# Writing the relative-bias rows from 96 partitions, and loading the compressed keys' bias from a table in steps of 16

## The chip, the core and the metric

One core of a Trainium2 chip runs the whole kernel. The metric is the device time of one execution in microseconds; lower is better. The core has TensorE (PE in the profile; PEld is its weight load), VectorE (DVE), ScalarE (ACT), GpSimd (POOL) and SyncE (SP), which here only issues DMAs: every DMA of this kernel stands in SP's one queue, in program order, and the transfers run on 16 DMA engines.

## The reference

Two decoder layers over 512 tokens of width 1024, batch 1, float32. Layer 0 is native sparse attention with 12 heads (compressed blocks, selected blocks, sliding window, gated and added) beside a 4-head cross-attention into `mem` (256 tokens); layer 1 is block-sparse attention with the same 12 heads beside the same kind of cross-attention. After each comes a gated convolutional FFN (width 2816). All softmax logits of the 12 heads get a bias that depends on the distance between query and key alone:

```python
def rel_bucket(dist):                  # 32 buckets over the distance
    ...
lg = einsum('bqgjd,bngd->bqgjn', qc, k_cmp) * scale + head_bias(rel_bucket(dist_c))   # 31 compressed keys
p_c = masked_softmax(lg, (dist_c >= 0)...)      # dist_c = t - (16 n + 31)
lg = einsum('bqgjd,bgqkd->bqgjk', qc, ks) * scale + bias_s                             # 512 keys
...
x = layer_norm(ALPHA * x + mix, ...)
```

The bias table `rel_bias` is 32 buckets x 12 heads. A compressed key n ends at position 16 n + 31, and there are 31 of them.

## The kernel before

It is written in a tile framework whose scheduler sets the order of the instructions on each engine from its own estimate of their times; priorities and buffers decide, not the order of the code alone. Every float32 product is made of three matmuls on values split in a high and a low part (`mm3`): ACT makes the high part (`hi`, line 231), DVE or POOL the low part (`lo`, lines 234 and 262). Weights come in units of 128 x 512 float32 (256 KB) into the tile `raw`, of which there are 5 (`unit`, lines 257 and 259), and are split from there.

How the bias gets to the logits: `tables` multiplies a one-hot matrix (33 x 640; row 32 stands for keys in the future) with `rel_bias`, once for the 12 heads, which gives one row of 640 values for each head, and ACT copies it to the tile `rt` (12 partitions, in a `kj` buffer). `bias_out` writes each row 32 times to `bias_rows` in DRAM (12 x 32 x 640 float32, 983 KB), by one DMA that reads each of the 12 partitions 32 times. `bias_tile` then loads, for a head, a tile `T` of 128 x 512 in which each partition's row is shifted by one: four DMAs of 32 partitions, 64 KB each (line 357). In layer 0, `cmp_bias` loads such a tile for each of the 12 heads as well, only to copy every 16th column of it (31 columns) on POOL into the table `C`, which `compressed_group` adds to the logits of the compressed keys (line 350).

The start of the program, in which all of this lies: x is transposed (`nat`, line 245), the K and V inputs of the compression are projected (`psS<-xh`), `stacked` copies them to two `p` tiles, the weights of V and of the gates (164 columns, tiles `p`, `v`, `pc`) are split, K is projected (`psmm<-xh`, 128 x 512) and then V and the gates in four blocks of tokens (`psmm<-p,xh`, later `psS<-p,xh`, 24 matmuls each). `mem_kv` transposes `mem` in two halves (`kj<-in_mem_dram`, two loads of 512 KB; high and low part in the tile `o`) and makes K and V of the cross-attention (`psS<-o,hi` and `psS<-hi,o`) from 8 weight units. `compress` runs twice over 8 units each (`in_a_cmp_w_k_dram`, `in_a_cmp_w_v_dram`; `psPT<-hi,p`). Then come the two cross-attention pairs (`psS<-xh,hi`, 24 matmuls of 512 columns) and the 12 heads of layer 0. The call order in `layer0` is: `compress` for K, gates, `compress` for V, `bias_out`, `cmp_bias` for 12 heads, `mem_pair`.

Of the kernel before, what the change touches and what calls it, by code (L numbers as in the profile page):

```python
# [10 lines left out]
F = mybir.dt.float32  # L11
R = mybir.dt.float32r
I32 = mybir.dt.int32
AF = mybir.ActivationFunctionType
# [7 lines left out]
NH = 12  # L22
# [11 lines left out]
GC = math.sqrt(2.0 / math.pi)  # L34
NREV = 640
REP = 32
OFF = (0, 128, 384, 768)


def _bucket(n):  # L40
    n = np.maximum(n, 0)
    nf = np.maximum(n, 1).astype(np.float32)
    large = 16 + (np.log(nf / np.float32(16)) / np.float32(math.log(128 / 16))
                  * np.float32(16)).astype(np.int32)
    return np.where(n < 16, n, np.minimum(large, 31))


def _onehot():
    dist = 511 - np.arange(NREV)
    oh = np.zeros((33, NREV), np.float32)  # L50
    oh[np.where(dist >= 0, _bucket(dist), 32), np.arange(NREV)] = 1.0
    return oh


SBUF = dict(raw=(5, 512), hi=(4, 1024), lo=(4, 1024), nat=(4, 1024), xh=(1, 4096), xl=(1, 4096),
# [127 lines left out]
class Trunk:  # L183
# [118 lines left out]

    def setup(self):
        nc, a = self.nc, self.a
        self.oh = self.al("kj")
        self.rb = self.one.tile([33, NH], F, name="rb")
        nc.vector.memset(self.rb[32:33, :], -BIG)
        self.nat = [self.al("nat") for _ in range(NT)]
        x = lambda tb, c0, c1: nc.sync.dma_start(self.nat[tb][:, c0:c1], a["x"][0, tb * 128:tb * 128 + 128, c0:c1])
        x(0, 0, 512)  # L310
        x(0, 512, D)
        nc.sync.dma_start(self.rb[0:32, :], a["rel_bias"])
        nc.sync.dma_start(self.oh[0:33, 0:NREV], a["onehot"])
        self.wkv = self.al("kj")
        nc.sync.dma_start(self.wkv.rearrange("p (k m) -> p k m", k=KC),
                          a["a_w_in"][0][:, 768:896].rearrange("(k p) m -> p k m", p=128))
        for tb in range(1, NT):
            x(tb, 0, D)
        self.ident = self.one.tile([128, 128], F, name="ident")
        make_identity(nc, self.ident)  # L320
        self.i2 = self.one.tile([64, 32], F, name="i2")
        nc.vector.tensor_add(self.i2, self.ident[0:64, 0:32], self.ident[0:64, 32:64])
        self.cw = self.one.tile([128, 2, NF * 3], F, name="cw")
        self.cb = self.one.tile([128, 2, NF], F, name="cb")
        self.new_xT()
        for tb in range(NT):
            self.to_xT(tb)

    def tables(self):
        nc, oh, rb = self.nc, self.oh, self.rb  # L330
        rt = self.al("kj")[0:NH, 0:NREV]
        for c0, c1 in ((0, 512), (512, NREV)):
            ps = self.pj()
            self.mm(ps[0:NH, 0:c1 - c0], rb, oh[0:33, c0:c1], True, True)
            nc.scalar.activation(rt[0:NH, c0:c1], ps[0:NH, 0:c1 - c0], AF.Copy, scale=-1.0)
        self.B = self.dr.tile([NH, REP, NREV], F, name="bias_rows")
        self.rt = rt
        self.aux = self.al("v")
        self.C = self.aux[:, 0:NH * 56].rearrange("p (h j) -> p h j", h=NH)
        nc.gpsimd.memset(self.C[:, :, 31:56], BIG)  # L340

    def bias_out(self):
        nc, a = self.nc, self.a
        nc.sync.dma_start(self.B, self.rt.unsqueeze(1).to_broadcast([NH, REP, NREV]))
        nc.sync.dma_start(self.cw, a["conv_w"])
        nc.sync.dma_start(self.cb, a["conv_b"])

    def cmp_bias(self, h):
        t = self.bias_tile(h)
        self.nc.gpsimd.tensor_copy(self.C[:, h, 0:31], t[:, 16:512].rearrange("p (j s) -> p j s", s=16)[:, :, 15])  # L350

    def bias_tile(self, h, c0=0):
        t = self.al("T")
        for p in range(0, 128, REP):
            src = bass.AP(tensor=self.B.tensor, offset=self.B.offset + h * REP * NREV + 127 - p + c0,
                          ap=[[NREV - 1, REP], [1, 512 - c0]])
            self.nc.sync.dma_start(t[p:p + REP, c0:512], src)
        return t
# [40 lines left out]
    def causal(self, q2, k2, T, gate, v, O, start, stop, qs=range(NT)):  # L399
# [5 lines left out]
        P = self.al("p")  # L405
        L = {i: P[:, OFF[i]:OFF[i] + 128 * (i + 1)] for i in qs}
        nm, sm = self.small(4), self.small(4)
# [413 lines left out]
    def layer0(self):  # L821
        nc, a = self.nc, self.a
        w = a["a_w_in"][0]
# [19 lines left out]
        ps = self.projT2(self.pj(), (v3(sh, 128), v3(sl, 128)))  # L843
# [5 lines left out]
        for j in range(2):  # L849
            d = (slice(None), slice(None), slice(64 * j, 64 * j + 64))  # L850
            src = v3(raw[j], 128)[:, :, 0:64]
# [9 lines left out]
        ps = self.projT(self.pj(), (v3(kh, 128), v3(kl, 128)))  # L861
# [17 lines left out]
        for tb in range(NT):  # L879
            ps = self.pj()  # L880
            t = slice(128 * tb, 128 * tb + 128)
# [9 lines left out]
        nc.vector.memset(self.G[0:31, 0, :, 0], 0.0)  # L891
        self.compress(t2v, pev, a["a_cmp_w1_v"][0], w2v, False)
        self.bias_out()
        for h in range(NH):
            self.cmp_bias(h)
        self.mem_pair(K2m, V2m, wq0, 0)
        self.mem_pair(K2m, V2m, self.cols(w, 1316), 1)

        q = {}
# [157 lines left out]
```

## Time and profile before

| | |
|---|---|
| median of 3 runs | 1258.29 us (1257.38 to 1259.96) |
| the profiled execution's own time | 1259.36 us |
| its span (first to last instruction) | 1257.4 us |
| mean granted TensorE clock | 0.985 of full speed |
| PE / PEld / DVE / ACT / POOL busy | 96% / 82% / 67% / 50% / 19% of the span |
| moved by DMA | 142.73 MB, 114 GB/s over the span |

The span is what the trace covers; the device time holds 2.0 us more around it. PE's matmuls are pipelined and their ends are modelled, so that a busy PE may still run at half its clock or wait for little things; the trace's stretches show where.

### The profile page before, as it was taken

The page shows a single profiled execution, that of the slowest core. Times are in us where ns is not written, and L with a number is a line of the kernel's source. Part 1 is how long each engine was busy: PE and PEld are TensorE (multiplying, and loading weights), DVE is VectorE, ACT ScalarE, POOL GpSimd, SP SyncE. Part 2 cuts the span into 40 slices and gives each one's busy share as a digit, 9 for nine tenths or more (in the row PEclk, how much of TensorE's full clock was granted, in tenths as well). Part 3 has the DMA queues.
Part 4 walks back from the last instruction along what each step waited for, and adds up shares of the span by engine and source line. Part 5 has one row for each costly group of instructions (what it writes and reads, how often), then busy time and mean ns, then how long its engine had stood idle before and what let it go on. Part 6 is the DMA issues. An engine that isn't in the chain of part 4 may idle for free.

```text
span 1257.4 us, 18606 instructions
## 1 busy us (share of the span) xinstructions
PE 1210.6 (96%) x6304; PEld 1032.2 (82%) x6304; DVE 847.6 (67%) x1861; ACT 628.4 (50%) x1347; POOL 237.8 (19%) x332
## 2 busy tenths in 40 slices
PE   7789999999999999999999999998899999999996
PEld 6778788888888888888879888887888888888875
DVE  6446897998755566468695665548875556646967
ACT  6458776672533334336543876456253433433652
POOL 0245553552000000000002445334200000000004
PEclk9899999999999999999999999999899999999998
DMA  9782110321534544336513223234154344433531
GB/s 234 209 202 80 46 43 24 79 84 35 168 118 121 148 124 128 101 118 209 176 59 102 75 77 90 79 93 118 34 160 125 118 140 129 127 107 117 170 108 67
DMA packets 173944, 142.73 MB, mean 114 GB/s; under 512 B 11768, under 2 KB 142200, under 8 KB 173849
## 3 DMA queue, kind: packets, MB, share of 16 engines
q1 hardware_dynamic: 173848, 141.55, 38.6%
q8 instruction: 50, 0.82, 0.3%
q14 instruction: 46, 0.37, 0.1%
HBM read 138.42 MB, written 3.08 MB: 113 GB/s over the span
## 4 chain that ended last, share of the span: by engine, by line
PE 84%; DVE 7%; DMA 3%; ACT 3%; issue 1%; SPq 1%; POOL 0%; DVEq 0%; POOLq 0%; ACTq 0%
PE psmm L237 41%; PE psS L237 28%; PE psPT L237 6%; PE psO L237 4%; PE psPT L245 4%; DVE pt L234 1%; DMA kj<-in_mem_dram 1%; DVE p L412 1%; DMA raw<-in_ffn_w_out_dram 1%; DVE nat L672 1%; ACT p L417 1%; ACT kj L231 1%; DVE nat L679 1%; ACT pt L231 1%; DVE nat L622 1%
## 5 line engine op out<-in xcount | busy, mean ns | idle before, releaser
L231 ACT ACTIVATE hi<-raw 128x512 fp32r<-128x512 f32 x370 | 216.4, 624 | 286.9 <-PE psS L237 158.0
L262 DVE TENSOR_TENSOR lo<-raw,hi 128x512 fp32r<-128x512 f32 x270 | 178.8, 693 | 108.1 <-ACT hi L231 106.4
L237 PE MATMUL psmm<-xh,lo 128*128 128x512 f32 (+1 forms) x560 | 212.0, 379 | 0.0
L237 PE MATMUL psmm<-xh,hi 128*128 128x512 f32 (+1 forms) x560 | 211.8, 379 | 0.0
L237 PE MATMUL psmm<-xl,hi 128*128 128x512 f32 (+1 forms) x560 | 211.7, 378 | 0.0
L262 POOL TENSOR_TENSOR lo<-raw,hi 128x512 fp32r<-128x512 f32 x68 | 88.8, 1328 | 438.9 <-DVE st L638 357.2
L237 PE MATMUL psS<-xh,hi 128*128 128x512 f32 (+1 forms) x408 | 151.9, 373 | 2.6 <-ACT G L888 2.6
L237 PE MATMUL psS<-xl,hi 128*128 128x512 f32 (+1 forms) x408 | 151.3, 372 | 0.1
L237 PE MATMUL psS<-xh,lo 128*128 128x512 f32 (+1 forms) x408 | 151.1, 370 | 0.0
L237 PEld LDWEIGHTS psmm<-xh,lo 128*128 128x128 f32 x560 | 105.4, 188 | 18.9
L237 PEld LDWEIGHTS psmm<-xl,hi 128*128 128x128 f32 x560 | 105.4, 188 | 18.7
L237 PEld LDWEIGHTS psmm<-xh,hi 128*128 128x128 f32 x560 | 105.4, 188 | 18.7 <-DVE qq L365 0.2
L237 PE MATMUL psmm<-hi,kj 128*128 128x512 f32 x328 | 114.3, 401 | 3.2 <-ACT kj L231 2.2
L417 ACT ACTIVATE p<-p,s 128x128 f32<-128x128 f32 (+3 forms) x144 | 79.9, 556 | 33.4 <-DVE s L412 32.6
L421 POOL TENSOR_SCALAR p<-p,s 128x128 f32<-128x128 f32 (+3 forms) x144 | 74.2, 532 | 99.7 <-DVE s L388 49.7
L237 PEld LDWEIGHTS psS<-xh,hi 128*128 128x128 f32 x408 | 77.8, 191 | 15.6 <-ACT G L888 2.8
L237 PEld LDWEIGHTS psS<-xl,hi 128*128 128x128 f32 x408 | 77.7, 191 | 13.4 <-DVE xl L234 0.5
L237 PEld LDWEIGHTS psS<-xh,lo 128*128 128x128 f32 x408 | 77.7, 190 | 13.0
L412 DVE CUSTOM_DVE_ANT_0 p<-psS,T 128x128 f32<-128x128 f32 (+3 forms) x144 | 66.1, 484 | 24.0 <-PE psS L237 20.5
L234 DVE TENSOR_TENSOR pt<-psPT,pt 128x512 fp32r<-128x512 f32 (+2 forms) x124 | 73.5, 606 | 8.4 <-ACT pt L231 7.6
L231 ACT ACTIVATE pt<-psPT 128x512 fp32r<-128x512 f32 (+2 forms) x124 | 64.1, 530 | 27.1 <-PE psPT L245 15.2
L237 PEld LDWEIGHTS psmm<-hi,kj 128*128 128x128 f32 x328 | 61.5, 189 | 16.1 <-ACT kj L231 2.6
(331 smaller groups left out, 2334.4 us busy)
## 6 DMA issues: line engine op xcount, KB each, us to landing
raw<-in_ffn_w_in_dram SPq DMA_DIRECT2D x176, 256.0 KB, 3.2
raw<-in_ffn_w_out_dram SPq DMA_DIRECT2D x152, 256.0 KB, 3.0
T<-bias_rows SPq DMA_DIRECT2D x144, 64.0 KB, 2.0
raw<-in_shared_w_kv_dram SPq DMA_DIRECT2D x24, 256.0 KB, 3.2
raw<-in_a_w_out_dram SPq DMA_DIRECT2D x16, 256.0 KB, 3.0
raw<-in_b_w_in_dram SPq DMA_DIRECT2D x16, 256.0 KB, 3.2
raw<-in_b_w_out_dram SPq DMA_DIRECT2D x16, 256.0 KB, 3.1
raw<-in_a_w_in_dram SPq DMA_DIRECT2D x14, 256.0 KB, 3.8
```

The source lines that it names most:

```text
L231: self.nc.scalar.activation(dst, src, AF.Copy)
L234: self.nc.vector.tensor_sub(dst, src, hi.bitcast(F))
L237: self.nc.tensor.matmul(o, l, r, start=start, stop=stop, skip_group_check=more)
L245: self.nc.tensor.transpose(o, i, self.ident)
L262: eng.tensor_sub(l[:, c], raw, h[:, c].bitcast(F))
L412: nc.vector.tensor_tensor_reduce(L[i], dst[i], T[:, 384 - 128 * i:512], op0=ALU.add, op1=ALU.min, scale=1.0, scalar=BIG, accum_out=nm[:, i ...
L417: nc.scalar.activation(L[i], L[i], AF.Exp, bias=nm[:, i:i + 1], scale=-1.0, accum_out=sm[:, i:i + 1])
L421: nc.gpsimd.tensor_scalar(L[i], L[i], r[:, i - qs[0]:i - qs[0] + 1], 1.0, op0=ALU.mult, op1=ALU.mult)
L622: nc.vector.scalar_tensor_tensor(self.nat[tb][:, sl], self.nat[tb][:, sl], ALPHA if first else 1.0, ps, op0=ALU.mult, op1=ALU.add)
L672: nc.vector.scalar_tensor_tensor(x[:, c], x[:, c], mu, gt[:, c], op0=ALU.subtract, op1=ALU.mult)
L679: eng.scalar_tensor_tensor(x[:, c], x[:, c], y, bt[:, c], op0=ALU.mult, op1=ALU.add)
```

## The change

The one-hot table gets 608 more columns: 16 groups of 38, in which column n of group m stands for the distance 511 - (46 - m + 16 n), so that a row of it is the bias in steps of 16. `tables` now makes two things: the rows as before, but for 96 columns of weights (each head 8 times, `rbs`, copied by DVE), so that they lie on 96 partitions; and for the 12 heads the 608 values in steps of 16, in two `pt` buffers. `bias_out` writes the latter to DRAM (`bias_16`, two DMAs from 12 partitions, 29 KB), writes `bias_rows` from 96 partitions with 4 copies of each, and loads the table `C` by 8 DMAs (16 partitions each, 12 heads x 31 values, runs of 124 bytes). `cmp_bias` is gone, with its 48 loads of `T` and 12 copies on POOL. The one-hot matrix moves from a `kj` to a `p` buffer.

```diff
--- before.py
+++ after.py
@@ -34,6 +34,8 @@
 GC = math.sqrt(2.0 / math.pi)
 NREV = 640
 REP = 32
+COPIES = 8
+NCMP = 38
 OFF = (0, 128, 384, 768)
 
 
@@ -49,7 +51,8 @@
     dist = 511 - np.arange(NREV)
     oh = np.zeros((33, NREV), np.float32)
     oh[np.where(dist >= 0, _bucket(dist), 32), np.arange(NREV)] = 1.0
-    return oh
+    by_16 = 46 - np.arange(16)[:, None] + 16 * np.arange(NCMP)
+    return np.concatenate([oh, oh[:, by_16.reshape(-1)]], 1)
 
 
 SBUF = dict(raw=(5, 512), hi=(4, 1024), lo=(4, 1024), nat=(4, 1024), xh=(1, 4096), xl=(1, 4096),
@@ -302,7 +305,7 @@
 
     def setup(self):
         nc, a = self.nc, self.a
-        self.oh = self.al("kj")
+        self.oh = self.al("p")
         self.rb = self.one.tile([33, NH], F, name="rb")
         nc.vector.memset(self.rb[32:33, :], -BIG)
         self.nat = [self.al("nat") for _ in range(NT)]
@@ -310,7 +313,7 @@
         x(0, 0, 512)
         x(0, 512, D)
         nc.sync.dma_start(self.rb[0:32, :], a["rel_bias"])
-        nc.sync.dma_start(self.oh[0:33, 0:NREV], a["onehot"])
+        nc.sync.dma_start(self.oh[0:33, 0:NREV + 16 * NCMP], a["onehot"])
         self.wkv = self.al("kj")
         nc.sync.dma_start(self.wkv.rearrange("p (k m) -> p k m", k=KC),
                           a["a_w_in"][0][:, 768:896].rearrange("(k p) m -> p k m", p=128))
@@ -328,26 +331,37 @@
 
     def tables(self):
         nc, oh, rb = self.nc, self.oh, self.rb
-        rt = self.al("kj")[0:NH, 0:NREV]
-        for c0, c1 in ((0, 512), (512, NREV)):
-            ps = self.pj()
-            self.mm(ps[0:NH, 0:c1 - c0], rb, oh[0:33, c0:c1], True, True)
-            nc.scalar.activation(rt[0:NH, c0:c1], ps[0:NH, 0:c1 - c0], AF.Copy, scale=-1.0)
+        n, m = NH * COPIES, 16 * NCMP
+        rbs = self.one.tile([33, NH, COPIES], F, name="rbs")
+        nc.vector.tensor_copy(rbs, rb.unsqueeze(2).to_broadcast([33, NH, COPIES]))
+        self.rt = self.al("kj")[0:n, 0:NREV]
+        self.ru = self.al("pt")[0:NH], self.al("pt")[0:NH, 0:m - 512]
+        for dst, w, c in ((self.rt[:, 0:512], rbs, 0), (self.rt[:, 512:NREV], rbs, 512),
+                          (self.ru[0], rb, NREV), (self.ru[1], rb, NREV + 512)):
+            if w is rbs:
+                w = rbs.rearrange("p h r -> p (h r)")
+            ps = self.pj()[0:dst.shape[0], 0:dst.shape[1]]
+            self.mm(ps, w, oh[0:33, c:c + dst.shape[1]], True, True)
+            nc.scalar.activation(dst, ps, AF.Copy, scale=-1.0)
         self.B = self.dr.tile([NH, REP, NREV], F, name="bias_rows")
-        self.rt = rt
+        self.B16 = self.dr.tile([NH, m], F, name="bias_16")
         self.aux = self.al("v")
         self.C = self.aux[:, 0:NH * 56].rearrange("p (h j) -> p h j", h=NH)
         nc.gpsimd.memset(self.C[:, :, 31:56], BIG)
 
     def bias_out(self):
         nc, a = self.nc, self.a
-        nc.sync.dma_start(self.B, self.rt.unsqueeze(1).to_broadcast([NH, REP, NREV]))
+        n = REP // COPIES
+        nc.sync.dma_start(self.B16[:, 0:512], self.ru[0])
+        nc.sync.dma_start(self.B16[:, 512:16 * NCMP], self.ru[1])
+        nc.sync.dma_start(self.B.rearrange("h (r n) c -> (h r) n c", n=n),
+                          self.rt.unsqueeze(1).to_broadcast([NH * COPIES, n, NREV]))
+        for q in range(8):
+            src = bass.AP(tensor=self.B16.tensor, offset=self.B16.offset + 7 - q,
+                          ap=[[NCMP, 16], [16 * NCMP, NH], [1, 31]])
+            nc.sync.dma_start(self.C[16 * q:16 * q + 16, :, 0:31], src)
         nc.sync.dma_start(self.cw, a["conv_w"])
         nc.sync.dma_start(self.cb, a["conv_b"])
-
-    def cmp_bias(self, h):
-        t = self.bias_tile(h)
-        self.nc.gpsimd.tensor_copy(self.C[:, h, 0:31], t[:, 16:512].rearrange("p (j s) -> p j s", s=16)[:, :, 15])
 
     def bias_tile(self, h, c0=0):
         t = self.al("T")
@@ -891,8 +905,6 @@
         nc.vector.memset(self.G[0:31, 0, :, 0], 0.0)
         self.compress(t2v, pev, a["a_cmp_w1_v"][0], w2v, False)
         self.bias_out()
-        for h in range(NH):
-            self.cmp_bias(h)
         self.mem_pair(K2m, V2m, wq0, 0)
         self.mem_pair(K2m, V2m, self.cols(w, 1316), 1)
```

The scheduler gives the start of the program another order. SP's queue before, from the write of the bias rows on (`kj_364` is the second half of `mem`, `T_857` the first head's tile for `cmp_bias`):

```order
L344 DMA bias_rows<-kj_209 384x1x640
L345 DMA cw<-in_conv_w_dram 128x132
L346 DMA cb<-in_conv_b_dram 128x44
L448 DMA kj_364<-in_mem_dram 128x1024
L257 DMA raw_475<-in_a_w_mem_kv_dram 128x2x256
L357 DMA T_857<-bias_rows 32x512 x2
L257 DMA raw_481<-in_a_w_mem_kv_dram 128x2x256
L357 DMA T_857<-bias_rows 32x512
L257 DMA raw_485<-in_a_w_mem_kv_dram 128x2x256
```

SP's queue now, from the first of the three bias writes on (`bias_227` is `bias_16`, `kj_375` the second half of `mem`, `v_228` holds the table `C`, `T_1259` and `T_1482` are the tiles of the first two attention heads):

```order
L355 DMA bias_227<-pt_212 12x512
L356 DMA bias_227<-pt_213 12x96
L357 DMA bias_rows<-kj_211 384x1x640
L363 DMA cw<-in_conv_w_dram 128x132
L364 DMA cb<-in_conv_b_dram 128x44
L462 DMA kj_375<-in_mem_dram 128x1024
L260 DMA raw_486<-in_a_w_mem_kv_dram 128x2x256
L362 DMA v_228<-bias_227 16x12x31
L260 DMA raw_492<-in_a_w_mem_kv_dram 128x2x256
L260 DMA raw_496<-in_a_w_mem_kv_dram 128x2x256
L362 DMA v_228<-bias_227 16x12x31 x7
L371 DMA T_1259<-bias_rows 32x512
```

The loads of `T` between the weight units are gone but for those of heads 0 and 1; two small writes stand ahead of the large one, and eight loads of `C` stand ahead of the units of the compression.

ACT before, from the split of the weights of V and the gates back to the copies of `stacked` (`p_279`, `p_282`; `p_287` is the split weight, `o_347` the transposed `mem`, `raw_382` and on the units of `mem_kv`):

```order
L231 ACTIVATE p_279<-psS_230 64x512
L231 ACTIVATE p_279<-psS_230 64x511
L231 ACTIVATE p_282<-psS_230 64x512
L231 ACTIVATE p_282<-psS_230 64x511
L231 ACTIVATE p_287<-kj_225 128x8x64
L231 ACTIVATE p_287<-kj_226 128x8x64
L231 ACTIVATE p_287<-v_217 128x8x36
L231 ACTIVATE o_347<-psPT_350 128x4x128
L231 ACTIVATE hi_380<-raw_382 128x512
L231 ACTIVATE o_347<-psPT_357 128x4x128
L231 ACTIVATE hi_380<-raw_386 128x512
```

ACT now, at the same place (`p_290`, `p_293` and `p_298` are the same three tiles, `o_358` the transposed `mem`, `raw_393` and on the same units):

```order
L234 ACTIVATE hi_391<-raw_393 128x512
L234 ACTIVATE o_358<-psPT_361 128x4x128
L234 ACTIVATE o_358<-psPT_368 128x4x128
L234 ACTIVATE hi_391<-raw_397 128x512
L234 ACTIVATE hi_435<-raw_437 128x512
L234 ACTIVATE p_290<-psS_241 64x512
L234 ACTIVATE p_290<-psS_241 64x511
L234 ACTIVATE p_293<-psS_241 64x512
L234 ACTIVATE p_293<-psS_241 64x511
L234 ACTIVATE p_298<-kj_236 128x8x64
L234 ACTIVATE p_298<-kj_237 128x8x64
L234 ACTIVATE p_298<-v_228 128x8x36
```

Five instructions that stood behind the split weight (two halves of the transposed `mem`, three weight units) stand ahead of the copies of `stacked` now; DVE's order is changed in the same way.

## Rows read from the trace of the kernel before

**Rows 1.** The page's first line and its chain of work that ended last, as shares of the span by engine.

```profile
span 1257.4 us, 18606 instructions
...
PE 84%; DVE 7%; DMA 3%; ACT 3%; issue 1%; SPq 1%; POOL 0%; DVEq 0%; POOLq 0%; ACTq 0%
```

**Rows 2.** The same chain in order of time, at the start of the program: start, duration (both us), what.

```profile
25.11 12.14 DMA kj<-in_mem_dram
...
60.76 6.03 DMA raw<-in_a_cmp_w_v_dram
...
68.97 7.29 PE psS L237 x24
```

**Rows 3.** Waits of PE between 18 and 100 us: engine, line, what it waited for, us in total, times, longest.

```profile
PE psPT L245 <- DMA kj<-in_mem_dram: 8.5, 1, 8.5
PE psS L237 <- ACT G L888: 2.6, 1, 2.6
PE psPT L237 <- ACT p L547: 0.8, 1, 0.8
PE psS L237 <- DVE kj L234: 0.5, 1, 0.5
```

**Rows 4.** Busy time in stretches of 2 us: stretch, its length, PE, PEld, DVE, ACT, POOL busy (x instructions), granted PE clock, DMA share of 16 engines, GB/s.

```profile
24.00:26.00 2.00, 2.00 (x10) 1.68 (x9) 2.00 (x7) 2.00 (x5) 0.00 (x0) 1.00 0.72 79
...
28.00:30.00 2.00, 0.85 (x8) 0.70 (x7) 2.00 (x5) 1.39 (x4) 0.00 (x0) 1.00 0.70 77
...
34.00:36.00 2.00, 0.00 (x0) 0.00 (x0) 0.00 (x0) 0.00 (x0) 0.00 (x0) 0.50 0.91 319
...
38.00:40.00 2.00, 2.00 (x10) 1.54 (x8) 0.86 (x2) 1.49 (x3) 0.00 (x0) 0.50 0.87 264
40.00:42.00 2.00, 2.00 (x11) 2.00 (x12) 1.66 (x3) 1.50 (x4) 0.23 (x1) 0.62 1.00 280
...
70.00:72.00 2.00, 2.00 (x6) 1.61 (x5) 0.76 (x6) 0.39 (x2) 0.23 (x1) 0.50 0.34 83
72.00:74.00 2.00, 2.00 (x9) 1.59 (x9) 0.00 (x0) 0.00 (x0) 0.23 (x1) 0.94 0.66 135
```

**Rows 5.** SP in order of time: start, duration, line, what it issued, how many.

```profile
15.05 4.19 SPq L257 DMA_DIRECT2D raw<-in_a_w_mem_kv_dram  x5
19.34 0.92 SPq L344 DMA_DIRECT2D bias_rows<-kj  x1
...
20.88 4.13 SPq L346 DMA_DIRECT2D cb<-in_conv_b_dram  x1
25.11 4.43 SPq L448 DMA_DIRECT2D kj<-in_mem_dram  x1
29.64 3.65 SPq L257 DMA_DIRECT2D raw<-in_a_w_mem_kv_dram  x1
34.56 0.80 SPq L357 DMA_DIRECT2D T<-bias_rows  x2
```

**Rows 6.** DMA issues between 34 and 76 us: what, how many, KB each, median us from issue to landing.

```profile
T<-bias_rows SPq DMA_DIRECT2D x48, 64.0 KB, 2.2
...
raw<-in_a_cmp_w_v_dram SPq DMA_DIRECT2D x8, 256.0 KB, 6.2
```

**Rows 7.** PE in order of time: start, duration of the row, what, [idle before]. The matmuls of the tables (x2: float32 goes through in two passes), the first transposes, the first block of V and the gates, the transposes of the second half of `mem`.

```profile
5.55 1.86 PE L237 MATMUL psS<-kj,rb 33*12 33x512 f32 x2
7.21 0.63 PE L237 MATMUL psmm<-kj,rb 33*12 33x128 f32 x2
8.69 2.82 PE L245 MATMUL psPT<-ident,nat 128*128 128x128 f32 x12 [0.84 <-DMA nat<-in_x_dram]
...
26.05 0.24 PE L237 MATMUL psmm<-p,xh 128*128 128x164 f32 x1
...
28.58 0.28 PE L237 MATMUL psmm<-p,xl 128*128 128x164 f32 x1
37.39 1.94 PE L245 MATMUL psPT<-ident,kj 128*128 128x128 f32 x8 [8.53 <-DMA kj<-in_mem_dram]
```

**Rows 8.** ACT in order of time, same columns: the copies of `stacked`, the split of the weights of V and the gates, weight units, K; and the last DVE instruction of that split.

```profile
19.89 2.42 ACT L231 ACTIVATE p<-psS 64x512 f32<-64x512 f32 x4 [1.01 <-PE psS L237]
22.34 1.16 ACT L231 ACTIVATE p<-kj 128x512 fp32r<-128x512 f32 x2
23.40 0.43 ACT L231 ACTIVATE p<-v 128x288 fp32r<-128x288 f32 x1
...
26.37 1.67 ACT L231 ACTIVATE hi<-raw 128x512 fp32r<-128x512 f32 x3
27.93 1.19 ACT L231 ACTIVATE kl<-psmm 64x512 fp32r<-64x512 f32 x2
...
24.96 0.28 DVE L234 TENSOR_TENSOR pc<-v,p 128x108 fp32r<-128x108 f32 x1
```

**Rows 9.** POOL's wait for the tiles of `cmp_bias`, between 28 and 80 us.

```profile
POOL v L350 <- DMA T<-bias_rows: 34.8, 12, 10.4
```

**Rows 10.** DMA issues from 15.9 to 16.4 us: what, how many, KB each, median us from issue to landing.

```profile
raw<-in_a_w_mem_kv_dram SPq DMA_DIRECT2D x2, 256.0 KB, 5.6
```

**Rows 11.** SP's issues of loads with short runs (L869: 256 bytes, L872: 64 bytes): start, duration, line, what, how many.

```profile
5.40 2.92 SPq L869 DMA_DIRECT2D v<-in_a_cmp_w_k_dram  x2
...
14.10 0.43 SPq L872 DMA_DIRECT2D v<-in_pe_v_dram  x1
```

## The prediction

> **What bounds the kernel now.** The chain of work that ended last is 84% PE [rows 1], so over the whole span the kernel is bound by matmuls, which this change does not touch but for the tables. What it can move is the start, where the same chain, read in order of time, leaves PE: 12.14 us on the load of the second half of `mem`, 6.03 us on weight units of the second compression [rows 2]. The waits of PE in that stretch say what this costs: 8.5 us for `mem`, then 0.8 and 2.6 us behind ACT, which stood in its own order behind weight units that had not landed, and 0.5 us behind DVE [rows 3].
>
> Why is `mem` late? SP issued the write of the bias rows at 19.34 us, and the first load that needs them starts at 34.56, when the write has landed: 15.2 us for 983 KB [rows 5]. While it alone is under way the DMA engines are busy 0.70 to 0.72, near 12 of 16, and move 77 to 79 GB/s; a stretch of loads right behind it has 319 GB/s [rows 4]. Behind the write, SP's next issues take 4.13, 4.43 and 3.65 us [rows 5], and the second half of `mem`, issued into this, takes the 12.14 us. After that come 48 loads of `T`, 3.1 MB, between the weight units [rows 6]; POOL waits 34.8 us for them [rows 9], which hurts nobody, but the units behind them are late, the ones of the second compression with 6.2 us to landing [rows 6].
>
> The waits also cost clock. PE is at half its clock (the granted clock is 0.50) when it comes back at 37.4, and the mean of 0.62 in 40 to 42 says that this lasts to about 41.5: 4.1 us of work at half speed, some 2.1 us lost. After the second wait the clock is 0.50 in 70 to 72 and 0.94 in 72 to 74, so from 68.97 to about 72.2: 1.6 us lost [rows 2, 4].
>
> **What the change removes.** The sum of the above, without the 0.5 us for DVE, which the change leaves: 8.5 (wait for `mem`) + 2.1 (clock) + 0.8 + 2.6 (waits behind ACT) + 1.6 (clock) = 15.6 us. Not all of the two waits behind ACT can go, since some latency of ACT and DVE stays once the units are there; I keep 0.7 of it. So 14.9 us are to be had if `mem` and the units come in time.
>
> Does `mem` come in time? The five units ahead of the write have landed by 17.9 + 5.6 = 23.5 us, with the last of them issued about 17.9 (1.35 us before SP's next row at 19.34) and the landing of their like [rows 5, 10]. How fast the write is from 96 partitions no row shows. Bounds: 983 KB at 319 GB/s, 3.1 us, and, if only the number of busy engines goes from 12 to 16, 78 x 16/12 = 104 GB/s, 9.5 us [rows 4]. Behind it 512 KB of `mem` need 1.6 us at 319 GB/s, so they land between 28 and 35 us. PE wants them behind the first block of V and the gates, which ends at 28.9 in the profile [rows 7] and, by what is added below, at about 31.5. I take the fast end, since the slow write's rate is far below anything that the engines do in the other stretches, and what is common to its packets is that 12 partitions are read 32 times each.
> [...]
>
> And the units? The 8 loads of `C` stand ahead of the compression's first unit, 190 KB in runs of 124 bytes. An issue of short runs took 0.43 us when the queue was free and 2.92 / 2 = 1.5 us when it was full [rows 11], so 3.4 to 12 us for all eight against 48 issues of `T` removed, at 0.80 / 2 = 0.4 us [rows 5] 19 us of SP and 3.1 MB / 319 GB/s = 9.9 us of transfer. SP comes to the compression's units at about 33 us then; ACT takes the first of them only behind K of the cross-attention, about 41. So the cover is some 5 us, and I put the loads of `C` at nothing.
>
> **What it adds and moves.** Two more matmul pairs for the table in steps of 16: by their likes 1.86 and, for 96 of 128 columns, 0.5 us; the 0.84 us that PE waits for x behind the tables take part of it [rows 7]. PE is then busy to 28.9 without a break, so 1.4 us later (bounds 1.2 and 2.4). ACT gets 0.7 us there, beside PE. The 80 KB more of one-hot table are 0.3 us of transfer, inside this.
>
> ACT and DVE are the price of the new order. Five ACT instructions now stand ahead of the copies of `stacked`, of which the last needs a unit that lands near 22.5; at 1.67 / 3 = 0.56 us each the copies start at about 23.4 instead of 19.89. The split weight is then ready on ACT at 27.3 instead of 23.83, and on DVE 1.4 us later, at 28.7 instead of 25.24 [rows 8]. PE comes to the first block that needs it at 26.05 + 1.4 = 27.5 [rows 7]: a new wait of 1.2 us (bounds 0.5 and 2.5). Behind it on ACT stand three units and one copy at 0.56 and K in two parts of 1.19 us, 4.6 us, before the transposed second half of `mem` [rows 8]: at 31.9 it begins, at 33 both halves are out, while PE is done with the transposes at 32.1. Another 1.0 us (bounds 0 and 2.5). Who waits behind: the cross-attention's K on PE, and all that follows.
>
> Sum: 14.9 - 1.4 - 1.2 - 1.0 = 11.3 us. Against the profiled execution's own 1259.4 us this is 1248.1; that run is 1.1 us over the median of the runs, from which it is 1247.0. I give 1247. From some 95 us on PE is full in both, and nothing there hangs on the bias but the tiles of the heads, of which each comes from DRAM as before; I take the gain to go through to the end.
>
> **The rivals.**
> - *The loads of `C` clog the queue* (the other side). If each issue is held as the ones behind the slow write were, about 4 us [rows 5], eight take 33 us instead of 3.4; SP comes to the compression's units at 62, PE waits for them from about 46 on, some 20 us against 11.3 gained: 1267. It turns at an issue of (11.3 + 5) / 8 + 0.4 = 2.5 us. Against it: 1.5 us is the dearest that a load of short runs took, in a full queue [rows 11]. [...]
> - *The write gets only 16/12 faster, or the new ACT and DVE order costs its upper bounds.* `mem` is 3 us later than PE wants it, and the clock may fall for another 1.5 us; or 2.5 + 2.5 us of new waits and the fallen clock. Gain 5 to 8: about 1251.
> - *The write is as slow as before* (the rows are read at the same rate, whatever the partitions): `mem` lands at 37 again, and what is left are the waits after it, 0.8 + 2.6 + 1.6 - 0.7 = 4.3, less 1.4 for the tables: 1255.4.
> - *All of it is won*: the tables hidden, no new wait on ACT: 14.9, 1243.4.
>
> **How the numbers follow.** My forecast (gain 9 to 14) 0.56; the second rival 0.22; the third 0.07; all won 0.06; the first, or another wait that eats the gain, 0.09. The range 1243 to 1254 leaves out the slow write, the clogged queue and the end of the best case, some 2 in 10. 0.2%, what a measurement of this kernel can tell, is 2.5 us. All cases but the last are faster by that, though the third barely: faster 0.89; same 0.04; slower 0.07.
>
> **What would show it.** Right: the write lands about 5 us after the units ahead of it, SP's issues behind it take under 1.5 us, PE's wait for `mem` is gone and the clock stays at 1.00 between 30 and 42; small new waits of PE behind DVE's `v` or ACT's `o` between 27 and 34; the first cross-attention pair (24 matmuls of 512) starts near 59 instead of 68.97 and takes 5.5 instead of 7.29 us. Wrong: a wait of PE for weight units of the compression, loads of `C` that take over 2 us to issue, a granted clock of 0.50 behind one of the new waits, or an early gain that is given back before 250 us.

## The result, and the profile after the change

| | before | after |
|---|---|---|
| device time, median | 1258.99 us (4 runs, 1257.38 to 1259.96) | 1247.49 us (4 runs, 1246.38 to 1248.12) |
| ratio | | 0.991, 95% interval 0.9894 to 0.9926 |
| profiled execution, own time | 1259.36 us | 1246.38 us |
| its span | 1257.4 us | 1244.6 us |

The change makes the kernel 11.5 us faster by the medians; 1247.0 was predicted. The two profiled executions lie 12.8 us apart in span, and all that follows on places is read from them.

The first lines of the page of the changed kernel, which answer to [rows 1]: span, and busy time, share of the span and instructions of PE.

```profile
span 1244.6 us, 18522 instructions
PE 1207.8 (97%) x6308; PEld 1029.9 (83%) x6308; DVE 847.2 (68%) x1862; ACT 629.2 (51%) x1349; POOL 235.0 (19%) x320
```

Waits of PE from 18 to 100 us, which answer to [rows 3]: engine, line, what it waited for, us in total, times, longest.

```profile
PE psS L240 <- DVE kj L237: 0.8, 1, 0.8
PE psS L240 <- ACT o L234: 0.8, 1, 0.8
PE psmm L240 <- DVE v L237: 0.6, 1, 0.6
```

The wait of 8.5 us for `mem` and the two behind ACT (2.6 and 0.8) are gone. Two of the three that are left are the new ones that the prediction named, behind the split weight `v` and behind the transposed `mem` in `o`; the third was there before with 0.5.

SP in order of time, as in [rows 5]: start, duration, line, what it issued, how many.

```profile
17.91 1.33 SPq L260 DMA_DIRECT2D raw<-in_a_w_mem_kv_dram  x1
...
20.18 0.68 SPq L357 DMA_DIRECT2D bias_rows<-kj  x1
...
21.57 1.81 SPq L364 DMA_DIRECT2D cb<-in_conv_b_dram  x1
23.47 1.38 SPq L462 DMA_DIRECT2D kj<-in_mem_dram  x1
24.95 0.38 SPq L260 DMA_DIRECT2D raw<-in_a_w_mem_kv_dram  x1
...
26.88 3.83 SPq L362 DMA_DIRECT2D v<-bias  x7
```

DMA issues between 18 and 34 us: what, how many, KB each, median us from issue to landing.

```profile
bias_rows<-kj SPq DMA_DIRECT2D x1, 960.0 KB, 6.5
...
cb<-in_conv_b_dram SPq DMA_DIRECT2D x1, 22.0 KB, 5.6
```

The write is issued at 20.18 and has landed at 26.7; it took 15.2 us before. The issues behind it, which took 4.13, 4.43 and 3.65 us, take 1.81, 1.38 and 0.38. The stretches of 2 us, with the columns of [rows 4], say the same from the side of the rate and of the clock:

```profile
24.00:26.00 2.00, 2.00 (x10) 1.69 (x9) 1.72 (x5) 1.94 (x5) 0.00 (x0) 1.00 1.06 293
26.00:28.00 2.00, 1.63 (x8) 1.13 (x6) 2.00 (x7) 2.00 (x6) 0.00 (x0) 1.00 0.82 298
...
32.00:34.00 2.00, 1.40 (x12) 1.40 (x13) 1.97 (x4) 1.21 (x3) 0.61 (x1) 1.00 0.63 160
...
40.00:42.00 2.00, 1.26 (x11) 1.10 (x10) 1.10 (x3) 1.48 (x5) 0.40 (x1) 1.00 0.48 145
...
sum 36.00, PE 33.84 PEld 32.23 DVE 24.41 ACT 23.91 POOL 4.15; mean PE 2.12 PEld 2.01 DVE 1.53 ACT 1.49 POOL 0.26
```

293 and 298 GB/s stand where 77 to 79 stood, and the granted clock, 0.50 from 32 to 40 before, is 1.00 throughout. The sum is over 24 to 60 us: PE is idle for 36.00 - 33.84 = 2.16 us there, the three waits above (0.83 + 0.77 + 0.56).

The chain that ended last, in order of time, as in [rows 2]:

```profile
42.09 5.98 PE psS L240 x48
...
57.77 5.67 PE psS L240 x24
```

The first cross-attention pair, at 68.97 with 7.29 us before, starts 11.2 us earlier and is 1.6 us shorter: 12.8 us are won by its end, and the span ends 12.8 us earlier. In between, the first FFN begins at 301.8 instead of 315.5 and the last output goes out at 1241.8 instead of 1254.6. So the gain is 13.7 us at the FFN, and 0.9 of it is lost again by the end: 0.3 by a longer wait of PE at the end of the second FFN (1.17 us for 0.84), the rest I did not trace.

### The profile page after: what moved, and what is told of

The parts are those of the page before. It is cut to its first block, busy times and chain, and to the rows that moved or that the text cites. A ratio compares the mean times of both kernels' runs of the same rounds, so it can differ in the third digit from the quotient of the medians.

```text
span 1244.6 us, 18522 instructions
## 1 busy us (share of the span) xinstructions
PE 1207.8 (97%) x6308; PEld 1029.9 (83%) x6308; DVE 847.2 (68%) x1862; ACT 629.2 (51%) x1349; POOL 235.0 (19%) x320
## 3 DMA queue, kind: packets, MB, share of 16 engines
q1 hardware_dynamic: 173260, 138.70, 37.4%
## 4 chain that ended last, share of the span: by engine, by line
PE 87%; DVE 7%; ACT 3%; DMA 1%; issue 1%; POOL 0%; SPq 0%; DVEq 0%; ACTq 0%; POOLq 0%
PE psmm L240 42%; PE psS L240 29%; PE psPT L240 7%; PE psO L240 5%; PE psPT L248 4%; DVE pt L237 1%; DMA raw<-in_ffn_w_out_dram 1%; DVE p L426 1%; DVE nat L686 1%; ACT p L431 1%; DVE xl L237 1%; DVE nat L693 1%; ACT pt L234 1%; DVE nat L636 1%; DVE st L652 0%
## 5 line engine op out<-in xcount | busy, mean ns | idle before, releaser
L431 ACT ACTIVATE p<-p,s 128x128 f32<-128x128 f32 (+3 forms) x144 | 79.9, 556 | 32.8 <-DVE s L426 31.9
L240 PEld LDWEIGHTS psS<-xh,hi 128*128 128x128 f32 x408 | 77.2, 189 | 12.6
L234 ACT ACTIVATE pt<-psPT 128x512 fp32r<-128x512 f32 (+2 forms) x124 | 64.2, 531 | 27.3 <-PE psPT L248 15.4
```

Of the source, the lines that this page charges most:

```text
L234: self.nc.scalar.activation(dst, src, AF.Copy)
L240: self.nc.tensor.matmul(o, l, r, start=start, stop=stop, skip_group_check=more)
L431: nc.scalar.activation(L[i], L[i], AF.Exp, bias=nm[:, i:i + 1], scale=-1.0, accum_out=sm[:, i:i + 1])
```

## The experiments

The landmark in the table is the start of the first pooling matmuls behind that pair (`psPT<-p,v`). "Landed" is the time from the issue of the bias write to the landing of the small load of the convolution's bias issued behind it (issue of `cb`, plus its time to landing, less the issue of the write), for which all but one of the kernels have rows. Ratios are against runs of the kernel before on the same chip; their medians were 1256.84 us for the first group (the two halves, 24 partitions, 12 that lie 8 apart), 1259.71 for the last two rows, 1257.67 for 48 partitions, 1258.21 for the other two.

| kernel | device time, us | ratio, 95% | landed, us | landmark, us |
|---|---|---|---|---|
| before | 1258.99 | 1 | 15.5 | 76.10 |
| after | 1247.49 | 0.991 (0.9894 to 0.9926) | 7.0 | 63.27 |
| write alone | 1250.31 | 0.9947 (0.993 to 0.9965) | 7.9 | 68.14 |
| table alone | 1259.34 | 1.0018 (1.0007 to 1.0029) | 15.5 | 74.71 |
| 24 partitions | 1251.23 | 0.995 (0.9935 to 0.9966) | 9.0 | 68.96 |
| 48 partitions | 1253.15 | 0.9963 (0.9949 to 0.9977) | 8.7 | 69.33 |
| 12 partitions, 8 apart | 1251.73 | 0.9954 (0.9939 to 0.9969) | 9.3 | 69.48 |
| 12 partitions, 9 apart | 1247.34 | 0.9912 (0.9895 to 0.9929) | 7.0 | 63.70 |
| 24 partitions, 0 to 11 and 32 to 43 | 1258.40 | 1.0001 (0.9991 to 1.001) | 14.8 (of `cw`) | 75.19 |
| 24 loads of `C` | 1250.81 | 0.9926 (0.9908 to 0.9944) | 6.5 | 66.72 |
| table in steps of 16 made late | 1255.41 | 0.997 (0.9959 to 0.9981) | 8.1 | 66.49 |

"Landed" is to be compared between kernels with the same order ahead of the write; the write alone and the late table have another one, and with it 7.9 and 8.1 from 96 partitions. The trace's semaphore records, which none of the views shown here prints, give the landing of the write itself. Counted from the landing of the last weight unit ahead of it, the write took 11.0 us before, and 11.9 and 11.7 in two profiles of the table alone; 5.2 from 24 partitions, 5.0 from 48 and 5.6 from 12 that lie 8 apart; 3.2 in the changed kernel and from 12 that lie 9 apart, 2.9 with 24 loads of `C`, 3.4 in the write alone and 3.5 with the late table. Counted so, the other order makes no exception.

### One half of the change alone

The write alone: the write from 96 partitions stays, the table in steps of 16, its two writes and the loads of `C` go, and the twelve `cmp_bias` with their loads of `T` come back. The order of the engines is that of the kernel before.

```diff
-        self.B16 = self.dr.tile([NH, m], F, name="bias_16")
-        for q in range(8):
...
+        for h in range(NH):
+            self.cmp_bias(h)
```

> The write of the bias rows from 96 partitions alone; the compressed keys' bias comes through the 48 loads of T and the copies on POOL, as before the change. The order of the engines is then that of the kernel before. Theory A (the slow write held back the second half of mem): the write takes 3 to 4 us behind the units ahead of it, PE's 8.5 us wait for mem and the half clock behind it (2.1 us) are gone, while the two waits behind the compression's units (0.8 + 2.6 and 1.6 of clock) mostly stay, since the loads of T still stand between the units: about 10 us won, 1248 to 1250. Rival B (the 48 loads of T are what crowds the start, the write matters little): 2 us won or less, 1256 to 1258.

Waits of PE from 18 to 100 us:

```profile
PE psPT L240 <- ACT p L556: 3.8, 1, 3.8
...
PE psPT L248 <- DMA kj<-in_mem_dram: 0.2, 1, 0.2
```

The wait for `mem` is gone but for 0.2 us, so the write alone has cured it. The wait behind ACT's `p`, which stands behind the units of the second compression, has stayed and grown from 0.8 + 2.6 to 3.8: with 48 loads of `T` between the units, PE, which now comes earlier, waits at that place for them. Behind it the clock is at 0.50 from 58 to 64. At the landmark 8.0 of the 12.8 us are won, and 6.5 by the medians; I had expected about 10.

The table alone: the rows are written from 12 partitions again; all else, the order of the engines too, is that of the changed kernel.

```diff
-        nc.sync.dma_start(self.B.rearrange("h (r n) c -> (h r) n c", n=n),
-                          self.rt.unsqueeze(1).to_broadcast([NH * COPIES, n, NREV]))
+        nc.sync.dma_start(self.B, self.rt.unsqueeze(1).to_broadcast([NH, REP, NREV]))
```

> The table in steps of 16 alone; the bias rows are written from 12 partitions, 32 times each, as before. The instructions stand on every engine in the order of the changed kernel, so that only the write differs from it. Theory A: the write takes 12 to 13 us again (77 to 79 GB/s), mem lands near 38, PE waits 6 to 7 us for it and loses 2 us of clock; the waits behind the compression's units are gone: 4 us won against the kernel before, 1254 to 1256. Rival B: the 48 loads were the cost, 9 to 11 us won, 1248 to 1250.

The waits of PE from 18 to 100 us, and then stretches of 2 us:

```profile
PE psPT L248 <- DMA kj<-in_mem_dram: 6.3, 1, 6.3
PE psS L240 <- ACT o L234: 1.3, 1, 1.3
PE psmm L240 <- DVE v L237: 0.9, 1, 0.9
```

```profile
34.00:36.00 2.00, 0.00 (x0) 0.00 (x0) 0.00 (x0) 0.00 (x0) 0.00 (x0) 0.51 0.75 189
...
46.00:48.00 2.00, 2.00 (x12) 2.00 (x12) 0.00 (x0) 0.00 (x0) 0.00 (x0) 0.58 0.18 52
...
1212.00:1214.00 2.00, 0.00 (x0) 0.00 (x0) 1.12 (x2) 1.78 (x4) 0.00 (x0) 1.00 0.01 4
1214.00:1216.00 2.00, 1.95 (x7) 1.56 (x8) 2.00 (x5) 1.56 (x3) 0.00 (x0) 0.76 0.02 4
1216.00:1218.00 2.00, 2.00 (x6) 1.60 (x5) 0.61 (x2) 0.00 (x0) 0.00 (x0) 0.50 0.00 0
```

I had expected a gain and there is none. At the landmark only 1.4 us are won: the wait for `mem` is 6.3 instead of 8.5, since PE comes to it later, and the waits behind the units are gone; but the tables, the two new waits and a clock that stays at half from about 34 to 47 (32 to 41.5 before) take most of it. The last three rows show where this profile loses the rest. At the end of the second layer's FFN, PE stands still for 2.09 us for the last weight loads (0.84 in the kernel before), and the clock then goes to 0.50.

To see whether that belongs to the kernel, the same kernel was profiled once more.

> The kernel with the table alone, once more, for a second profile. In its first profile it was 1.7 us ahead of the kernel before at the first FFN (313.8 against 315.5), and lost 3 us at the end of the second layer's FFN, where TensorE stood still for 2.09 us (0.84 in the kernel before) for the last weight loads, and the granted clock then fell to 0.50. Theory A (the head's gain of this half is small but there, and the end's loss comes with it nearly always, since the time was above that of the kernel before in all but a few of ten runs): the wait at 1211 to 1214 is again 1.8 to 2.3 us with a fall of the clock behind it, span 1257.5 to 1259.5. Rival (the end's wait changes from execution to execution): it is 0.8 to 1.5 us, the clock stays at 1.00 there, and the span is 1255 to 1256. In both the wait for the memory is 6.0 to 6.6 us and the clock is 0.50 from about 34 to 46.

PE in order of time at that place, second profile:

```profile
1212.70 0.50 PE L240 MATMUL psPT<-hi,kj 128*128 128x512 f32 x1 [0.89 <-ACT kj L234]
```

This time PE waited 0.89 us there, the clock stayed at 1.00 and the span was 1255.9 us, as the rival has it: the end's loss changes from one execution to the next. The head was much the same in both (7.1 us for `mem`, more than either theory allowed, and the landmark at 74.64). The table alone is worth about 1.5 us at the landmark. In the timed runs it came out 0.2% slower than the kernel before (1.0007 to 1.0029); the two profiles, whose spans lie 1.2 us over and 1.5 us under that of the kernel before, do not explain this.

### What sets the rate of the write

24 partitions instead of 96 (`COPIES = 2`), and 12 partitions 8 apart:

```diff
-COPIES = 8
+COPIES = 2
```

> The changed kernel with 2 copies of each row on 24 partitions instead of 8 on 96, each read 16 times; the orders are those of the changed kernel. If the number of partitions (or of ways into them) sets the rate, the write runs at about 156 GB/s and takes 6.3 us behind the units, mem lands near 31 and PE waits for it 0 to 1.5 us: 1247.5 to 1249.5. If only the number of DMA engines that share it counts, 24 rows divide by 12 and not by 16, the rate stays at 77 to 79 GB/s and the time is that of the write from 12 partitions, 1254 to 1256.

```diff
-        nc.sync.dma_start(self.B.rearrange("h (r n) c -> (h r) n c", n=n),
-                          self.rt.unsqueeze(1).to_broadcast([NH * COPIES, n, NREV]))
+        nc.sync.dma_start(self.B, self.rt[0:NH * COPIES:COPIES, :].unsqueeze(1).to_broadcast([NH, REP, NREV]))
```

> The changed kernel, but the write reads 12 partitions only, every eighth of the 96 (0, 8, ... 88), 32 times each; the orders are those of the changed kernel. If what limits is the single partition, read 32 times, or the 12 engines, the write runs at 77 to 79 GB/s as from partitions 0 to 11, 1254 to 1256. [...]

First a stretch of 2 us and a wait of PE from 18 to 100 us of the 24 partitions, then stretches of the 12 that lie 8 apart, and their waits of PE and (from 22 to 42 us) of ACT:

```profile
26.00:28.00 2.00, 1.62 (x8) 1.13 (x6) 2.00 (x6) 2.00 (x5) 0.00 (x0) 1.00 0.86 178
...
PE psS L240 <- ACT o L234: 2.4, 1, 2.4
```

```profile
26.00:28.00 2.00, 1.13 (x6) 0.57 (x4) 2.00 (x7) 2.00 (x5) 0.00 (x0) 1.00 0.73 182
...
36.00:38.00 2.00, 2.00 (x13) 2.00 (x13) 0.29 (x2) 0.20 (x1) 0.00 (x0) 0.59 0.84 273
38.00:40.00 2.00, 2.00 (x11) 2.00 (x11) 0.00 (x0) 0.00 (x0) 0.00 (x0) 0.50 0.96 279
40.00:42.00 2.00, 2.00 (x11) 2.00 (x10) 0.00 (x0) 0.00 (x0) 0.00 (x0) 0.50 0.19 53
42.00:44.00 2.00, 2.00 (x14) 2.00 (x14) 0.00 (x0) 0.40 (x1) 0.00 (x0) 0.71 0.03 8
...
PE psS L240 <- ACT o L234: 2.8, 1, 2.8
...
ACT hi L234 <- DMA raw<-in_a_w_mem_kv_dram: 2.7, 1, 2.7
```

The kernel before had a DMA share of 0.70 to 0.72 while it moved 77 to 79 GB/s; with 12 partitions 8 apart the share is 0.73 at 182 GB/s. At nearly the same share more than twice as much was moved, so twelve engines were not the limit. For the 24 partitions I had expected 1247.5 to 1249.5 at a rate like this one; they came out at 1251.23, and the 12 that lie 8 apart at 1251.73, though `mem` was late by 0.4 us at most. The last rows show why. A weight unit of `mem_kv`, issued behind the slow write, keeps ACT waiting for 2.6 us (24 partitions) and 2.7 us, and the copies to `o` stand behind that unit in ACT's order; the changed kernel has no such wait. With PE's wait behind `o` at 2.4 and 2.8 us instead of 0.8, the clock falls: with 12 partitions 8 apart, by the shares of 0.59, 0.50, 0.50 and 0.71 PE runs at half its clock for 1.6 + 2 + 2 + 1.2 = 6.8 us of the eight, 3.4 us lost. The waits are longer by 3.2 us (2.0 behind `o`, 0.3 behind `v`, and 0.9 behind `G`, against the changed kernel). That makes 6.6; PE came to the first of them 0.5 us earlier than in the changed kernel, which leaves 6.1 of the 6.2 us at the landmark.

48 partitions, 0 to 47 (`COPIES = 4`):

> The changed kernel with the bias rows written from 48 partitions (4 copies) instead of 96; the order of all engines is that of the changed kernel. Theory A (the rate of the write grows with how many partitions it reads, 77 to 79 GB/s from 12, 167 to 178 from 24): 48 lies by 250 to 330 GB/s with the other loads, the small load of the convolution's bias behind it lands 6 to 6.5 us after its issue (5.6 with 96, 7.4 with 24), the wait for ACT `o` is 0.8 to 1.3 us, the granted clock stays at 1.00 from 30 to 42 or dips for a short stretch, time 1247 to 1249, FFN of the first layer starts at 302 to 304. Rival (beyond 24 partitions the number makes no difference, and 96 gained by something else): the wait for ACT `o` stays at 2.4 us, the clock falls to 0.50 by 38, time 1251, FFN at 307.5.

As the rival has it: it landed in 8.7 us, so like 24 and not between 24 and 96, the wait behind `o` was 2.1 us, the clock 0.50 from 36 to 42, and the first FFN began at 308.5. Twice as many partitions gave next to nothing (8.7 us for 9.0), and 12 that lie 8 apart did about as well (9.3) as 24 that touch. So the places of the partitions were to be told apart from their number. That the places count was my estimate, from 9.3 us for 12 partitions 8 apart against 15.5 for 12 side by side; by the rivals it is the number. Two kernels were to put this to the test, with the rest of the changed kernel left as it is: 12 partitions 9 apart, and 24 of which the second half lies 32 behind the first.

```diff
-COPIES = 8
+COPIES = 9
```

(a change to the kernel with 12 partitions 8 apart, which are then 0, 9, ... 99)

> The kernel with 12 partitions spread over the memory, now 9 apart (0, 9, ..., 99) instead of 8 apart; everything else, the order of the engines too, is that kernel's. From the issue of the write to the landing of the small load of the convolution's bias behind it, the kernels so far took 15.5 us (12 partitions side by side), 9.0 (24), 8.7 (48), 9.3 (12, 8 apart) and 7.0 (96). [...] Rival B (12 partitions mean 12 of the 16 DMA engines, and these set what is left): 9 to 9.5 us as with 8 apart, wait 2.4 to 2.8, half clock from 36 to 43, time 1251 to 1252.

```diff
-        rbs = self.one.tile([33, NH, COPIES], F, name="rbs")
+        rbs = self.one.tile([33, COPIES, 32], F, name="rbs")
...
+        for r in range(COPIES):
+            nc.sync.dma_start(self.B[:, r * n:r * n + n, :],
+                              self.rt[32 * r:32 * r + NH, :].unsqueeze(1).to_broadcast([NH, n, NREV]))
```

(a change to the changed kernel, with `COPIES = 2`)

> The changed kernel with the bias rows written from 24 partitions that lie in two groups of 12, at 0 to 11 and at 32 to 43, by two issues of 480 KB instead of one; the rest, the order of the engines too, is that of the changed kernel. [...] Rival B (the number of partitions counts): as the 24 side by side, 9 us, 167 to 178 GB/s, 1251 to 1252.

12 partitions 9 apart: stretches of 2 us, and PE's waits from 18 to 100 us.

```profile
26.00:28.00 2.00, 1.72 (x8) 1.07 (x6) 2.00 (x6) 2.00 (x5) 0.00 (x0) 1.00 1.02 361
```

```profile
PE psmm L240 <- DVE v L237: 0.9, 1, 0.9
...
PE psS L240 <- ACT o L234: 0.8, 1, 0.8
```

24 partitions, the second 12 of them 32 behind the first: the same two views.

```profile
26.00:28.00 2.00, 1.73 (x9) 1.23 (x7) 2.00 (x7) 2.00 (x6) 0.00 (x0) 1.00 0.73 80
```

```profile
PE psPT L248 <- DMA kj<-in_mem_dram: 5.9, 1, 5.9
PE psS L240 <- ACT o L234: 1.3, 1, 1.3
```

The first fell on the side of the places. Twelve partitions 9 apart are as good as 96 (7.0 us, against the rival's 9 to 9.5; 0.9912 against 0.991), and twelve 8 apart are not (9.3 us, 0.9954), though their number is the same. The semaphore records show a difference inside the write as well. The landing of a write from 12 partitions is told there by twelve updates (sixteen with 48 and with 96 partitions), besides one that comes within 1.4 us of the issue. With 8 apart, four of the twelve come at 26.1 us and eight at 28.6 to 29.1. With 9 apart all twelve come between 26.5 and 27.3. The records do not name the partition, so which eight were late, and why, is not shown.

Twenty-four in two groups that lie 32 apart are as slow as twelve side by side (80 GB/s, 5.9 us for `mem`, 1.0001), against the rival's 9 us, but this kernel does not decide between places and number. It writes by two issues, and they ran one after the other: the first half had landed at 28.3 us, the second at 34.9, 6.6 us later, 75 GB/s for 480 KB. Each half alone is a write from twelve neighbours, which ran at 77 to 79 GB/s in the kernel before. That the places count rests on the kernels with one issue: 12 side by side, 8 apart and 9 apart (15.5, 9.3 and 7.0 us), and 48 against 24 (8.7 and 9.0).

### The loads of `C`, and the table on PE

24 loads of `C` instead of 8 (each made three times over), against the rival in which they clog the queue:

```diff
-        for q in range(8):
+        for q in 3 * tuple(range(8)):
```

> The changed kernel with the 8 loads of the table C issued three times over (24 loads, the last ones count); ACT, DVE and PE keep their orders, SP gets 16 issues more ahead of the compression's units. My cover for these loads was about 5 us of SP: at 0.45 us an issue the 16 more take 7.2 us, so the first unit of the compression is issued near 39 instead of 31.75 and lands near 42.5, 1 us after ACT wants it (41.4): 0 to 2 us slower than the changed kernel, 1247.5 to 1249.5. The rival that these loads clog the queue (2.5 us an issue or more when there are many in flight) says 16 x 2.5 = 40 us of SP and over 20 us slower.

SP in order of time, and PE's wait between 46 and 66 us:

```profile
34.85 7.58 SPq L362 DMA_DIRECT2D v<-bias  x14
```

```profile
PE psPT L240 <- ACT p L561: 1.4, 1, 1.4
```

A load took 7.58 / 14 = 0.54 us to issue, where the rival needed 2.5, so the rival is refuted. The cost was more than the 0 to 2 us that I had expected, 3.4 us at the landmark, since behind the new wait of 1.4 us the clock fell (0.50 and 0.69 in 60 to 64) and the pair took 7.31 us instead of 5.67. In the timed runs, which spread from 1246.56 to 1254.88, the interval overlaps that of the changed kernel.

The table in steps of 16 made late: its two matmul pairs are taken from the head and put where the scheduler likes, behind the cross-attention's weights.

```diff
-        for dst, w, c in ((self.rt[:, 0:512], rbs, 0), (self.rt[:, 512:NREV], rbs, 512),
-                          (self.ru[0], rb, NREV), (self.ru[1], rb, NREV + 512)):
+        for dst, c in ((self.rt[:, 0:512], 0), (self.rt[:, 512:NREV], 512)):
...
+        self.steps_of_16()
```

> The changed kernel, with the table in steps of 16 made late: its one-hot columns lie in a tile of their own (a T and an ot buffer), the two matmul pairs, the writes and the 8 loads of C come behind the second compression, ahead of the first head. By this the 1.8 us of table matmuls leave PE's start, and in the new order ACT has one weight unit instead of five instructions ahead of the copies of stacked. Theory: the 1.3 us by which PE comes late to the first block of V and the gates, and most of the two new waits (0.6 and 0.8 us), are gone, 1 to 2.5 us faster than the changed kernel: 1245 to 1246.5. Rival: what is taken off the start comes back as waits for mem or units, or the late loads of C hold back the first heads' tiles: 1247 or more.

Stretches of 2 us:

```profile
30.00:32.00 2.00, 1.02 (x7) 0.58 (x5) 2.00 (x5) 1.98 (x5) 0.48 (x1) 1.00 0.82 221
32.00:34.00 2.00, 0.74 (x5) 0.74 (x5) 1.97 (x4) 1.17 (x3) 0.45 (x1) 0.89 1.00 322
34.00:36.00 2.00, 2.00 (x11) 2.00 (x11) 0.10 (x1) 0.00 (x0) 0.61 (x1) 0.50 0.33 115
```

Slower than the changed kernel, where I had expected it to be 1 us faster. The tables moved from the head to 83.7 us, where they still cost PE their 1.1 us, and what was won there came back as two waits close together, 1.4 us behind ACT's `G` and 0.8 behind `o`; PE is busy for 1.02 and 0.74 us of two stretches, and the clock is at 0.50 from 34 to 40. At the landmark 3.2 us are lost; at the first FFN (310.5 against 301.8) 8.7. The clock falls a second time, to 0.72 and 0.50 from 118 to 122, behind two waits of DVE's `s` of up to 0.9 us; the rest of the loss between the two places I did not trace.

## Why the prediction was right, point by point

**The waits that go.** All of the 8.5 + 0.8 + 2.6 us of waits and the 2.1 + 1.6 us of clock are gone, the 15.6 us of the sum. The two halves of the change have one of them each: the write alone takes away the wait for `mem` and keeps the one behind the units (3.8); the table alone takes away the one behind the units and keeps that for `mem` (6.3). That is why 8.0 and 1.4 us at the landmark make 12.8 together: behind the wait that is left the clock still falls to 0.50, and each half alone pays for it (with the write alone from 58 to 64; with the table alone PE works at half its clock from 37.4 to about 47.7, where it was to 41.5 before: some 2 us more lost).

**The write.** I took the fast end of 3.1 to 9.5 us. By the semaphore records the last unit ahead landed at 23.5 and the write at 26.7, 3.2 us later, where the prediction's sign said about 5. Of SP's issues behind it, which were to take under 1.5 us, one took 1.81. The reason given for it ("12 partitions are read 32 times each") pointed at the right thing, the reading side, but not at what counts there: twelve partitions 9 apart, read as often, are as fast as 96 (7.0 us both). The upper bound rested on a misreading. The busy share of 0.70 to 0.72 was taken for a limit of 12 engines, and the second rival with it; the kernel with 12 partitions 8 apart has 0.73 at more than twice the rate (182 GB/s for 77 to 79).

**The tables.** 1.4 us predicted; the gates start at 27.39 instead of 26.05, 1.34 us later. PE in order of time, the four rows of the tables, as in [rows 7]:

```profile
6.03 1.99 PE L240 MATMUL psS<-p,rbs 33*96 33x512 f32 x2 [0.61 <-DVE xl L237]
7.81 0.63 PE L240 MATMUL psmm<-p,rbs 33*96 33x128 f32 x2
8.37 1.88 PE L240 MATMUL psS<-p,rb 33*12 33x512 f32 x2
10.04 0.52 PE L240 MATMUL psmm<-p,rb 33*12 33x96 f32 x2
```

**The two new waits.** They came where they were predicted, and were smaller: 0.56 us for 1.2 behind the split weight, 0.77 for 1.0 behind the transposed `mem`. The first is the term that was most mis-sized. PE in order of time, and the last rows of DVE's split:

```profile
27.39 0.24 PE L240 MATMUL psmm<-p,xh 128*128 128x164 f32 x1
28.19 0.34 PE L240 MATMUL psmm<-v,xh 128*128 128x164 f32 x1 [0.56 <-DVE v L237]
...
29.93 0.28 PE L240 MATMUL psmm<-pc,xh 128*128 128x164 f32 x1
```

```profile
27.80 0.33 DVE L237 TENSOR_TENSOR v<-v,p 128x180 fp32r<-128x180 f32 x1
28.05 0.26 DVE L237 TENSOR_TENSOR pc<-v,p 128x108 fp32r<-128x108 f32 x1
```

The prediction let PE wait for the last instruction of the split (28.7 predicted, 28.31 in fact). But PE's second matmul needs only `v`, ready at 28.13; `pc`, the last, is read first at 29.93. Of the 0.64 us by which the term was too large, 0.39 are the split's earlier end and 0.18 are this. The second wait has the same fault: ACT's two copies to `o` ran from 31.95 to 33.04, as predicted (31.9 to 33), but PE went on at 32.60, before the second was done.

**The sum.** By the measured terms, 15.6 - 1.34 - 0.56 - 0.77 - 0.3 (the wait behind `kj`, 0.8 for 0.5) = 12.6 of the 12.8 us. The prediction had 11.3: 0.9 us too much for the two new waits, and 0.4 us too much for what stays of the old ones. That the median was met within 0.5 us all the same is in part luck: the sum was 1.5 us short of the 12.8 between the two profiles, but 1.1 us were taken off because the profiled execution of before lay over its median, and the one of after happens to lie 1.1 us under its own (1246.38 against 1247.49), so that the medians are only 11.5 us apart. The two errors cancel in part.

**The rivals.** That `C` clogs the queue is refuted by 0.54 us an issue; a slow write by the landing of it; the limit of 12 engines by the two kernels with 12 partitions apart. That all is won (14.9) was 2.1 us too high by the profiles; the tables and the two new waits took 2.7.

## What to carry to other kernels

The large write from twelve neighbouring partitions ran here at a fraction of the rate (77 to 79 GB/s, where loads had 319) and held up what was issued behind it (SP's next issues took 4.13, 4.43 and 3.65 us): try such a write from partitions that are spread, and look at places, not at the number alone (twelve 9 apart were as fast as 96). The busy share of the DMA engines did not show this limit (0.70 to 0.73 at 77 and at 182 GB/s), the GB/s beside it did. When two waits stand one behind the other, try both cures together before judging either: here the clock fell to 0.50 behind the one that was left and ate part of the other's gain (8.0 and 1.4 us alone, 12.8 together). And of a wait for a tile made in pieces, ask which piece is read first.

## What the runs showed of the hardware that was not expected

- How long the write took depended on which partitions it read, not on their number alone. The rows give 15.5 us for 12 partitions side by side, 8.7 to 9.3 for 24, 48 and 12 that lie 8 apart, and 6.5 to 7.0 for 96 and for 12 that lie 9 apart. From the first of these to the second 15.5 - 9.0 = 6.5 us are won, from the second to the third some 2. What the partitions of a slow write have in common no run shows. At 3.2 us behind the units ahead the write runs at 983 / 3.2 = 307 GB/s, near the 319 GB/s of the loads in [rows 4], so that something else than the places may hold it there, or the loads of `mem` and of the units that share the DMA engines; neither was tried.
- A short standstill cost nearly twice its length in one profile. In the first one of the table alone 2.09 us without work at 1212 were followed by a granted clock of 0.76, 0.50 and, in 1218 to 1220, 0.89: half clock for 1.0 + 2 + 0.4 us, so 1.7 us more lost. The kernel before, with 0.84 us at that place, kept 1.00, and so did the one with 24 partitions, with 1.52. But 1.4 us in the kernel with 24 loads of `C` were followed by 0.50 and 0.69, so the length of the wait alone does not tell. In the 12 partitions 8 apart, 3.2 us of longer waits came with 3.4 us lost to the clock.
- PE's wait for the last weight loads of the second FFN was between 0.65 and 2.09 us in eleven of the twelve profiles, and missing in the write alone; the same kernel had 2.09 and 0.89. A difference of 1 to 3 us in span between two single profiles can come from there alone.
